# A PSUM ring kept through the next stage, whole first loads and one more weight buffer in a two-layer encoder step

## The chip, the cores and the metric

The kernel runs on one core of one Trainium2 chip. The metric is the time of one execution on the device in microseconds. Five engines matter: TensorE (PE, with PEld for its weight loads), VectorE (DVE), ScalarE (ACT), GpSimd (POOL) and SyncE (SP), which issues most DMAs. Each engine works through its own instructions strictly in the order in which the program gives them; semaphores hold an instruction until what it needs is there. The order on each engine is written by the kernel itself.

## The reference

One inference step of an encoder trunk of two layers, for 1024 prompt frames and 32 sample frames (1056 columns together), with model width 1024. All numbers are 32-bit floats.

```python
# layer 0
q, k, v, o, ig, fg = split(x @ w_in)
mix = mlstm(q, k, v, ig, fg) * g_norm * sigmoid(o) @ w_out      # 8 heads, chunks
x = layer_norm(alpha * x + mix)
x = layer_norm(alpha * x + (silu(x @ w_g) * (x @ w_u)) @ w_down)
# layer 1
k_sh, v_sh = x @ w_kv
mix = windowed_attention(x @ w_q, k_sh, v_sh, sinks, alibi) @ w_out   # 16 heads
x = layer_norm(alpha * x + mix)
x = layer_norm(alpha * x + (silu(x @ w_g) * (x @ w_u)) @ w_down)
```

The inner width of the SwiGLU layer is 2816. Outputs are x for both groups, the final states of the recurrence and the last window rows of keys and values.

## The kernel before

**Products.** A product of 32-bit numbers is made on TensorE from two halves of each operand: a rounded part (hi) and the rest (lo), with three matmuls per 128-row tile, hi x hi, hi x lo and lo x hi (`gemm`, lines 365 to 367). For weights the halves are called wh and wl, for activations both lie in `SX` (sx), with further room in `E` (ex). Columns are worked in three groups of 384, 384 and 288 (`GRP`) in the projections, and in four quarters of 264 (`QUARTERS`) around the layer norms and the SwiGLU layers.

**Weights.** The class `Weights` holds a list of units of 128 x 1024 numbers in order of use. Each unit is loaded by SP into one of three raw buffers (`wr`, `RAW`), then each of its two factors is split: ScalarE writes wh (line 206), and GpSimd, or VectorE for the factors in the set `on_vector`, writes wl (line 208). Split factors live in `SLOTS` buffers (tags wh and wl), except those that have a `home` elsewhere. `live` counts the buffers in use. `done` gives a factor's buffer back and splits on until `SLOTS - 1` are in use; where `ahead` is set, `feed` splits one more whenever a buffer is free and 1.7 us of planned matmul time have passed. After the last factor of a unit `load_to` orders the next raw load, on SP's queue at that place.

In the SwiGLU layers, pairs of units are combined: seven factors a1, a2, b2, s2, s1, s3, s4 come from two units and from sums of their parts that VectorE makes in place in the raw buffers (lines 179 to 185); each is used by 24 matmuls on sums of the activations. The seven products use them in the order a1, a2, s2, b2, s1, s3, s4. Up products (`up_tile`) add into bank pairs A and B of PSUM, which ScalarE copies out (lines 1356, 1366, 1373, 1384) and VectorE adds up (lines 1361, 1369, 1376 to 1378). The intermediate is split and stored to DRAM by `stage` (lines 1282 to 1284) and loaded back for the down products (`load`, line 1433). Down products (`down`) work through five blocks; VectorE adds each bank into `ACT` (act, the activations) at lines 1485 and 1487. `stage`, the loads and the norms are tasks (`Weave`) that advance with the planned time of the matmuls.

**The end of a SwiGLU layer.** The last block of the down product is plain: for each quarter eight products (`run` in `ffn`), each into one PSUM bank out of a ring of five (`dense_psum(5)`, `psbank`), added to act by VectorE at line 1547. Behind each quarter runs a layer norm task (`ln_task`): VectorE sums over tiles (lines 603 and 605), a matmul with a matrix of 1/1024 gives the mean (line 426), VectorE centres (431), ScalarE squares (433), VectorE and GpSimd sum up (435, 438), a second such matmul gives the variance (442), ScalarE takes logarithm, exponential and square (448 to 450), VectorE finishes the scale (452, 453), scales (456), ScalarE or VectorE apply gain and bias (464, 462) and the halves are made (470, 476). After the last quarter of layer 0 the norms of its third and fourth quarter are still running when the next stage begins.

**The next stage.** Layer 1 begins with the shared keys and values of the first column group (`keys_values(0)`: `k_group`, whose result ScalarE and VectorE split at lines 1581 and 1582, and `v_group`, line 1614) and four query projections (`q_group(j, 0)`, lines 1623 and 1624). Each takes one bank with `psbank`. In the kernel before, the ring of five is closed at the end of `ffn`, a ring of three opened, and two banks `psS` for the attention scores are taken right away, with a memset each (line 1661). The norm tasks hold three further banks on the other side of PSUM.

**The start.** SP loads the first half of the first weight unit (line 165), two of eight x tiles of the first column group (line 637), the second half (line 167), the other six, the second unit in halves, and then the other column groups (line 644). Each x tile is split by ScalarE and VectorE (lines 395 and 396). Twelve small matmuls run before (line 631). The first projections write q (ScalarE copies at line 697) and k, with a ring of three banks.

Of the kernel before, what the change touches and what calls it, by code (L numbers as in the profile page):

```python
# [9 lines left out]
F32 = mybir.dt.float32  # L10
# [3 lines left out]
PSUM = bass.MemoryType.PSUM  # L14
DRAM = bass.MemoryType.DRAM

P = 128
D = 1024
KT = D // P
# [21 lines left out]
NG = 2 * HEADS  # L41
WD = D + 4 * NG
RAW = 3
SLOTS = 5
GAP_M = (0.6, 1.666, 1.519, 1.5)
GAP_A = 0.46

# [15 lines left out]
GRP = ((0, 384), (384, 384), (768, 288))  # L63
# [65 lines left out]
class Weights:  # L129
# [21 lines left out]
                self.last[u] = len(self.jobs) - 1  # L151
                u += 1

    def load_to(self, i, between=None):
        while self.nload <= i and self.nload < len(self.units):
            u = self.nload
            ap = self.units[u]
            w = ap.shape[-1]
            r = self.pool.tile([P, WD], F32, name=f"wr{u}", tag="wr", bufs=RAW)
            self.raw[u] = r  # L160
            self.nload += 1
            if between is None:
                self.nc.sync.dma_start(r[:, :w], ap)
                continue
            self.nc.sync.dma_start(r[:, : w // 2], ap[:, : w // 2])
            between()
            self.nc.sync.dma_start(r[:, w // 2 : w], ap[:, w // 2 :])

    def _source(self, u, f):

# [17 lines left out]
    def _next(self):  # L188
# [3 lines left out]
        u, f = key  # L192
        if key not in self.home and len(self.live) == SLOTS:
            return False
# [7 lines left out]
        else:  # L202
            self.live.add(key)
            hi = self.pool.tile([P, WD // 2], F32R, name=f"wh{u}_{f}", tag="wh", bufs=SLOTS)[:, :w]
            lo = self.pool.tile([P, WD // 2], F32R, name=f"wl{u}_{f}", tag="wl", bufs=SLOTS)[:, :w]
        self.nc.scalar.copy(hi, r)  # L206
# [25 lines left out]
    def done(self, u, f=None):  # L232
        for k in (0, 1) if f is None else (f,):
            self.parts.pop((u, k))
            self.live.discard((u, k))
        while not self.ahead and len(self.live) < SLOTS - 1 and self.njob < len(self.jobs) and self._next():
            pass
# [9 lines left out]
def kernel(ctx: ExitStack, tc: tile.TileContext, A, O):  # L247
    nc = tc.nc
# [5 lines left out]
    def pool(name, space=None, side=None):  # L254
        kw = {}
        if space is not None:
            kw["space"] = space
        if side is not None:
            kw["side"] = side
        return tc.tile_pool(name=name, bufs=1, reuse_waits="tile", **kw)  # L260

    def new(p, tag, shape, dt=F32, bufs=1):
        uid[0] += 1
        return p.tile(list(shape), dt, name=f"{tag}_{uid[0]}", tag=tag, bufs=bufs)
# [6 lines left out]
    units, on_vector, pairs = [], set(), set()  # L271
# [12 lines left out]
    U_Q, U_K, U_V = [], [], []  # L284
# [31 lines left out]
    U_OUT_B = [[add("wout_b", u) for u in range(8)] for _ in range(2)]  # L316
    add_ffn(1)
    on_vector.update((u, f) for u in U_OUT_A[0] + U_OUT_B[1] for f in range(2))
    on_vector.update([(0, 0), (0, 1), (1, 0)])
    W = Weights(nc, base, units, pairs, on_vector)  # L320
    wv.feed = W.feed

# [16 lines left out]
    def views(t):  # L339

        return [[t[:, k, t0 : t0 + n] for t0, n in GRP] for k in range(KT)]

    act, sxh, sxl = views(ACT), views(SX[:, 0]), views(SX[:, 1])
# [5 lines left out]
    psx = [None, None]  # L349

    def dense_psum(bufs):
        psx[0] = ExitStack()
        psx[1] = psx[0].enter_context(pool("psd", PSUM)), bufs
# [16 lines left out]
    def psbank():  # L370
        return new(psx[1][0], "d", [P, 512], F32, bufs=psx[1][1])
# [22 lines left out]
    def split_act(k, g):  # L394
        nc.scalar.copy(sxh[k][g][:], act[k][g][:])  # L395
        nc.vector.tensor_sub(sxl[k][g][:], act[k][g][:], sxh[k][g][:].bitcast(F32))  # L396
# [194 lines left out]
    def norm_tail(li, run, box, final=False):  # L591


        tasks = []
        for g, (cols, (c, zs)) in enumerate(QUARTERS):

            def after(order, i):
                if i in (3, 5, 7):
                    if i == 3 and g > 1:
                        wv.drain(tasks[g - 2])  # L600
                    acc = box[0].z[:, 0:2, c, zs]
                    pair = [ACT[:, order[j] : order[j] + 2, cols] for j in (i - 1, 0)]
                    nc.vector.tensor_add(acc, acc if i > 3 else pair[1], pair[0])
                if i == KT - 1:
                    nc.vector.tensor_add(acc[:, 0], acc[:, 0], acc[:, 1])

            if final and g == 3:
                wv.drain(tasks[1])
                run(g, cols, None, LastNorm(box[0].z, box[0].lnps, QUARTERS[g], li))
                break  # L610
            run(g, cols, after)
            if g == 0 and li & 1:
                nc.scalar.preload_act_table_set("natural_log_exp_and_others")
            last = g >= 3
            tasks.append(wv.launch(ln_task(box[0].z, box[0].lnps, QUARTERS[g], li, last, final)))
            box[0].norms = tasks
        return tasks
# [13 lines left out]
        nc.tensor.matmul(warm[:, :P], onesm[:], onesm[:], start=True, stop=True)  # L631
    for g, (t0, n) in enumerate(GRP):
        if g == 0:

            def inputs(*ks):
                for k in ks:
                    nc.sync.dma_start(act[k][0][:], A["x"][:, k, : GRP[0][1]])

            W.load_to(0, lambda: inputs(0, 1))
            inputs(*range(2, KT))  # L640
            W.load_to(1, lambda: None)
        else:
            for k in range(0, KT, 2):
                nc.sync.dma_start(act_g[g][:, k : k + 2], A["x"][:, k : k + 2, t0 : t0 + n])
        if g == 2:
            W.load_to(2)
        if g == 0:
            gbias = pa.tile([40, 1], F32, name="gbias")
            sm0 = pa.tile([HEADS, 1], F32, name="sm0")
            nc.sync.dma_start(gbias[0:8], A["b_gate"][0:8])  # L650
            nc.sync.dma_start(gbias[32:40], A["b_gate"][8:16])
            nc.sync.dma_start(sm0[:], A["state_m"])
            gt = gp.tile([P, 9, NG], F32, name="gt")
            smask = gp.tile([HEADS, 384], F32, name="smask")
            sel = gp.tile([HEADS, PAIRS, P], F32, name="sel")
            cmask = pa.tile([P, P], F32, name="cmask")
            nc.sync.dma_start(smask[:], A["smask"])
            nc.sync.dma_start(ident[:], A["ident"])
    W.factor(0, 0)
    for g in range(3):  # L660
        for k in range(KT):
            split_act(k, g)
            if (g, k) == (0, 1):
                W.split_to(0)
        if g == 0:
            W.split_to(1)
    nc.sync.dma_start(sel[:], A["sel"])
# [564 lines left out]
    def ffn(layer, li, tasks, lx, final):  # L1232
# [283 lines left out]

        late = [(u, f) for u in dn[TAIL] for f in range(2)][SLOTS - 1 :]
        for b in range(TAIL):
# [11 lines left out]
        px.close()  # L1530
        W.ahead = True
        dense_psum(5)
        for _ in range(3):
            psbank()
        lx.lnps = lx.enter_context(pool("lnps", PSUM, side="right"))

        def run(g, cols, after, own=None):
# [13 lines left out]

        r = norm_tail(li, run, [lx], final)
        lx.ex.close()
        psx[0].close()
        dense_psum(3)
        return r

    def parts_made(g):
# [1 line left out]

    tasks, lx = mixer_out(U_OUT_A, 0, lx, None, lambda g: g < 3 and parts_made(g))
    tasks = ffn(0, 1, tasks, lx, False)

    eb = ExitStack()
    pb = eb.enter_context(pool("pb"))
    psb0 = eb.enter_context(pool("psb0", PSUM))
    psS = [psb0.tile([P, 512], F32, name=f"psS{h}") for h in range(2)]  # L1570
    KC = T + P
    KH = [pb.tile([P, KC], F32R, name=f"KH{g}") for g in range(2)]
    KL = [pb.tile([P, KC], F32R, name=f"KL{g}") for g in range(2)]
# [75 lines left out]
    def load_bias(j):  # L1649
        at, bufs = (pb2, 1) if j == 5 else (pb, 2)  # L1650
        bt = new(at, "bt", [P, 2, 257], bufs=bufs)
        sb = new(at, "sb", [DEC, 2, 161], bufs=bufs)
        nc.sync.dma_start(bt[:, :, 0:256], A["bias"][:, 2 * j : 2 * j + 2, :])
        nc.sync.dma_start(sb[:, :, 0:160], A["bias"][:DEC, 2 * j : 2 * j + 2, 0:160])
        nc.gpsimd.tensor_copy(bt[:, :, 256], nsink[:, 2 * j : 2 * j + 2])
        nc.gpsimd.tensor_copy(sb[:, :, 160], nsink[:DEC, 2 * j : 2 * j + 2])
        B[j] = (bt, sb)

    load_bias(0)
    for h in range(2):  # L1660
        nc.vector.memset(psS[h][:, 256:257], 0.0)
    def keys_values(g):
        if g == 2:
            k_part(ck[:], SEQ, P)
        for f, w in ((k_group, U_KV[g > 0][0]), (v_group, U_KV[g > 0][1])):
            f(g)
            if g != 1:
                W.done(w)
# [8 lines left out]
        wv.drain(t)  # L1677
    lx.close()
    lx.zx.close()

    pb2 = eb.enter_context(pool("pb2"))
    W.home[U_QB[1][5], 1] = [new(pb2, "oh", [P, D // 2], F32R, bufs=2)[:] for _ in range(2)]
# [177 lines left out]

    tasks, lx = mixer_out(U_OUT_B, 2, None, finish, before)
    ffn(1, 3, tasks, lx, True)
    while wv.tasks:
        wv.tick(0.25)
# [129 lines left out]
```

## Time and profile before

| | us |
|---|---|
| median of 3 runs | 2232.54 |
| lowest and highest | 2228.96, 2235.09 |
| the profiled execution | 2233.3 |
| its span, first to last instruction | 2231.5 |
| TensorE busy in it | 2184.5 |
| VectorE, ScalarE, GpSimd busy | 1452.1, 1000.8, 1042.2 |

Rows of a timeline give the start, the length, the engine, the line, the operation and the tiles (out<-in); rows that follow one another with the same form are merged (xN). In square brackets stands how long the engine was idle before it and what it waited for. In the list of waits each line has the waiting and the awaited operation, the total, the number of times and the longest. In the rows by stretch, each pair is busy time and number of instructions, and the granted clock is that of TensorE as a share of full speed. Matmuls overlap, so the length of a matmul row is longer than its distance to the next one.

### The profile page before, as it was taken

To read this page: it belongs to the slowest core of one execution; us is meant where nothing else is said; L and a number is where in the kernel's file an instruction comes from. 1 tells how busy PE (TensorE), PEld (TensorE's weight loads), DVE (VectorE), ACT (ScalarE), POOL (GpSimd) and SP (SyncE) were. 2 spreads that over 40 slices of the span, in tenths; PEclk is the share of its full clock that TensorE was granted. 3 is DMA by queue.
4 is the path that set the end of the run, shared out by engine and by line. 5 is a ranking of instruction groups with operands and counts; after the bars stand their busy time and mean duration, and the time that the engine had idled before them with its cause. 6 is when DMAs were issued, how large, how long until landed. Compare 5 with 4: busy or idle time off the path is not lost.

```text
span 2231.5 us, 44260 instructions
## 1 busy us (share of the span) xinstructions
PE 2184.5 (98%) x17086; PEld 2154.7 (97%) x17086; DVE 1452.1 (65%) x2833; ACT 1000.8 (45%) x2259; POOL 1042.2 (47%) x997
## 2 busy tenths in 40 slices
PE   9999999999999999999998999999999999999997
PEld 8899999999999999999998999899999999999997
DVE  4465577777566665566667678788666665456657
ACT  3443355455444444322235778756344444422225
POOL 2444331003666666544525776700566666554441
PEclk9999999999999999999999999999999999999999
DMA  4222112311443444697525433421244344398722
GB/s 150 74 55 66 51 38 93 98 39 58 165 139 141 154 145 144 217 331 237 177 69 168 115 103 86 141 79 40 100 167 155 134 144 157 125 332 270 238 72 79
DMA packets 174787, 298.10 MB, mean 134 GB/s; under 512 B 18096, under 2 KB 130792, under 8 KB 174576
## 3 DMA queue, kind: packets, MB, share of 16 engines
q1 hardware_dynamic: 170224, 290.94, 40.0%
q10 hardware_dynamic: 4352, 4.33, 0.6%
q8 instruction: 135, 2.21, 0.4%
q14 instruction: 76, 0.62, 0.1%
HBM read 201.80 MB, written 82.94 MB: 128 GB/s over the span
## 4 chain that ended last, share of the span: by engine, by line
PE 60%; DVE 5%; DMA 3%; ACT 3%; issue 2%; POOL 2%; SPq 0%; POOLq 0%; DVEq 0%; ACTq 0%
PE A L365 9%; PE A L367 9%; PE A L366 9%; PE B L365 6%; PE B L366 6%; PE B L367 6%; PE d L365 4%; PE d L367 4%; PE d L366 4%; DMA wr<-in_dn 1%; PE T L1759 1%; ACT act L464 1%; POOL s L1739 1%; PE O L1774 1%; PE O L1775 1%
## 5 line engine op out<-in xcount | busy, mean ns | idle before, releaser
L208 POOL TENSOR_TENSOR wl_s<-wr,wh_s 128x512 fp32r<-128x512 f32 x224 | 316.1, 1430 | 247.2 <-ACT wh_s L206 189.6
L365 PE MATMUL d<-sx,wh 128*128 128x264 f32 (+2 forms) x1068 | 343.4, 322 | 4.6 <-DVE act L1547 2.4
L367 PE MATMUL d<-sx,wl 128*128 128x264 f32 (+2 forms) x1068 | 326.9, 306 | 1.1 <-POOL wl L208 1.1
L366 PE MATMUL d<-sx,wh 128*128 128x264 f32 (+2 forms) x1068 | 326.7, 306 | 0.5 <-DVE sx L396 0.4
L208 POOL TENSOR_TENSOR wl_a<-wr,wh_a 128x512 fp32r<-128x512 f32 x112 | 168.3, 1510 | 327.7 <-ACT wh_a L206 325.6
L206 ACT CAST wh_s<-wr 128x512 fp32r<-128x512 f32 x224 | 135.6, 617 | 308.4 <-DVE wr L183 280.8
L365 PE MATMUL A<-sx,wh_s 128*128 128x264 f32 x896 | 254.9, 284 | 1.7 <-ACT z L1366 1.7
L366 PE MATMUL A<-sx,wh_s 128*128 128x264 f32 x896 | 254.2, 284 | 0.0
L367 PE MATMUL A<-sx,wl_s 128*128 128x264 f32 x896 | 254.0, 284 | 0.0
L365 PEld LDWEIGHTS d<-sx,wh 128*128 128x128 f32 x1068 | 203.3, 190 | 8.3 <-issue 2.6
L366 PEld LDWEIGHTS d<-sx,wh 128*128 128x128 f32 x1068 | 203.5, 191 | 2.5 <-DVE sx L396 1.5
L208 POOL TENSOR_TENSOR wl<-wr,wh 128x512 fp32r<-128x512 f32 (+2 forms) x94 | 123.1, 1318 | 177.1 <-ACT wh L206 174.5
L367 PEld LDWEIGHTS d<-sx,wl 128*128 128x128 f32 x1068 | 202.7, 190 | 2.0 <-POOL wl L208 1.7
L365 PE MATMUL d<-sx,ex 128*128 128x264 f32 x624 | 180.6, 289 | 0.4 <-ACT sx L395 0.2
L366 PE MATMUL d<-sx,ex 128*128 128x264 f32 x624 | 177.4, 284 | 0.4 <-DVE sx L396 0.2
L367 PE MATMUL d<-sx,ex 128*128 128x264 f32 x624 | 176.9, 284 | 0.0
L365 PEld LDWEIGHTS A<-sx,wh_s 128*128 128x128 f32 x896 | 168.4, 188 | 2.4 <-ACT z L1366 2.1
L367 PEld LDWEIGHTS A<-sx,wl_s 128*128 128x128 f32 x896 | 168.9, 188 | 0.0
L366 PEld LDWEIGHTS A<-sx,wh_s 128*128 128x128 f32 x896 | 168.4, 188 | 0.0
L1283 POOL TENSOR_TENSOR z<-z 128x528 fp32r<-128x528 f32 x76 | 104.4, 1373 | 110.4 <-ACT z L1282 103.7
L1739 POOL TENSOR_SCALAR s<-s,st 128x256 f32<-128x256 f32 (+1 forms) x144 | 123.0, 866 | 44.3 <-DVE st L1737 30.4
L1282 ACT CAST z<-z 128x528 fp32r<-128x528 f32 x136 | 85.8, 631 | 94.3 <-DVE z L1295 40.5
(347 smaller groups left out, 7292.7 us busy)
## 6 DMA issues: line engine op xcount, KB each, us to landing
wr<-in_gu SPq DMA_DIRECT2D x92, 512.0 KB
hs_x<-z SPq DMA_DIRECT2D x72, 528.0 KB
hs_t<-z SPq DMA_DIRECT2D x64, 528.0 KB
sx<-hs_x SPq DMA_DIRECT2D x112, 264.0 KB
sx<-hs_t SPq DMA_DIRECT2D x64, 264.0 KB
ex<-hs_t SPq DMA_DIRECT2D x64, 264.0 KB
wr<-in_dn SPq DMA_DIRECT2D x32, 512.0 KB
ex<-hs_x SPq DMA_DIRECT2D x32, 264.0 KB
```

What stands on the lines that cost most here:

```text
L206: self.nc.scalar.copy(hi, r)
L208: eng.tensor_sub(lo, r, hi.bitcast(F32))
L365: nc.tensor.matmul(out, ah, bh, start=start and k == 0, stop=False, **kw)
L366: nc.tensor.matmul(out, ah, bl, start=False, stop=False, **kw)
L367: nc.tensor.matmul(out, al, bh, start=False, stop=stop and k == last, **kw)
L464: nc.scalar.activation(z, z, AF.Identity, scale=gk, bias=bk)
L1282: nc.scalar.copy(hi.bitcast(F32R), buf(s))
L1283: eng.tensor_sub(lo.bitcast(F32R), buf(s), hi)
L1739: nc.gpsimd.tensor_scalar_mul(p[:R, h, lo:256], p[:R, h, lo:256], st[:R, 2, h : h + 1])
L1759: nc.tensor.transpose(pt[:nk, i, h, :R], p[:R, h, c : c + nk], ident[:R, :R])
L1774: nc.tensor.matmul(po[:, :, :R], v, s["hi"][:nk, i, :, :R], start=(i == 0), stop=False)
L1775: nc.tensor.matmul(po[:, :, :R], v, s["lo"][:nk, i, :, :R], start=False, stop=(i == len(kts) - 1))
```

## The change

Three edits go together.

- The ring of five banks is no longer closed at the end of `ffn`. It stays through the first key, value and query projections, and is closed after the norm tasks are done; then the ring of three is opened and `psS` taken and set. The three calls of `psbank` whose result nothing uses are gone.
- The first two weight units are each loaded by one DMA, the first ahead of all eight x tiles, the second behind them. Both factors of the first unit are split before the first x tile is. On VectorE are now the two factors of the first unit; the first factor of the second unit moves to GpSimd.
- `SLOTS` goes from 5 to 6: six buffers for wh and six for wl. With it `done` keeps five in use, and in the last block of the down product five factors, not four, lie in these buffers while one fewer gets a place in `E` (line 1517).

```diff
-SLOTS = 5
+SLOTS = 6
...
-    def load_to(self, i, between=None):
+    def load_to(self, i):
         while self.nload <= i and self.nload < len(self.units):
...
+            self.nc.sync.dma_start(r[:, :w], ap)
             self.raw[u] = r
             self.nload += 1
-            if between is None:
-                self.nc.sync.dma_start(r[:, :w], ap)
-                continue
-            self.nc.sync.dma_start(r[:, : w // 2], ap[:, : w // 2])
-            between()
-            self.nc.sync.dma_start(r[:, w // 2 : w], ap[:, w // 2 :])
...
-    on_vector.update([(0, 0), (0, 1), (1, 0)])
+    on_vector.update((u, f) for u in U_Q[:1] for f in range(2))
...
-            W.load_to(0, lambda: inputs(0, 1))
-            inputs(*range(2, KT))
-            W.load_to(1, lambda: None)
+            W.load_to(0)
+            for k in range(KT):
+                nc.sync.dma_start(act[k][g][:], A["x"][:, k, t0 : t0 + n])
+            W.load_to(1)
...
-    W.factor(0, 0)
+    W.split_to(0)
     for g in range(3):
         for k in range(KT):
             split_act(k, g)
-            if (g, k) == (0, 1):
-                W.split_to(0)
         if g == 0:
             W.split_to(1)
...
         dense_psum(5)
-        for _ in range(3):
-            psbank()
         lx.lnps = lx.enter_context(pool("lnps", PSUM, side="right"))
...
         lx.ex.close()
-        psx[0].close()
-        dense_psum(3)
         return r
...
-    psb0 = eb.enter_context(pool("psb0", PSUM))
-    psS = [psb0.tile([P, 512], F32, name=f"psS{h}") for h in range(2)]
...
-    for h in range(2):
-        nc.vector.memset(psS[h][:, 256:257], 0.0)
...
     lx.close()
     lx.zx.close()
+    psx[0].close()
+    dense_psum(3)
+    psb0 = eb.enter_context(pool("psb0", PSUM))
+    psS = [psb0.tile([P, 512], F32, name=f"psS{h}") for h in range(2)]
+    for h in range(2):
+        nc.vector.memset(psS[h][:, 256:257], 0.0)
```

More of the change, by code (lines that the diff above doesn't have):

```diff
@@ L633 @@
         if g == 0:
-            def inputs(*ks):
-                for k in ks:
-                    nc.sync.dma_start(act[k][0][:], A["x"][:, k, : GRP[0][1]])
-            W.load_to(0, lambda: inputs(0, 1))
-            inputs(*range(2, KT))
-            W.load_to(1, lambda: None)
+            W.load_to(0)
+            for k in range(KT):
+                nc.sync.dma_start(act[k][g][:], A["x"][:, k, t0 : t0 + n])
+            W.load_to(1)
         else:
```

## The prediction

> **What bounds the kernel now.** I read the page first, then the list of waits, then busy time by stretch, and last the timelines around each long wait of TensorE.
>
> ```profile
> span 2231.5 us, 44260 instructions
> PE 2184.5 (98%) x17086; PEld 2154.7 (97%) x17086; DVE 1452.1 (65%) x2833; ACT 1000.8 (45%) x2259; POOL 1042.2 (47%) x997
> ```
>
> TensorE is idle for 2231.5 - 2184.5 = 47 us. The change removes no matmul, so it can win only some of that, and the slow matmuls that follow a long pause. The waits name what it can reach:
>
> ```profile
> PE A L365 <- DVE act L1485: 3.3, 2, 1.7
> PE ln L442 <- DVE z L438: 2.8, 1, 2.8
> PE d L365 <- DVE act L1547: 2.4, 1, 2.4
> PE d L365 <- ACT qT L697: 1.8, 1, 1.8
> PE d L367 <- POOL wl L208: 1.1, 2, 0.6
> ...
> ACT wh_b L206 <- DMA wr<-in_dn: 21.7, 6, 4.5
> ...
> ACT wh_b L206 <- DMA wr<-in_gu: 6.9, 6, 2.0
> ```
>
> Columns: total us, times, longest. The third line is the PSUM bank that the first key projection waits for, the second the layer norm behind it, the first the start of the second down product, the fifth a weight half that came late. The stretches say where there is nothing to win, and what a pause costs afterwards:
>
> ```profile
> 560.00:960.00 400.00, 398.72 (x3280) 1.00 0.47 166
> ...
> 20.00:24.00 4.00, 2.18 (x13) 1.85 (x12) 2.52 (x7) 3.17 (x8) 2.14 (x6) 1.00 0.93 339
> 1182.00:1184.50 2.50, 2.50 (x9) 2.40 (x9) 1.20 (x4) 0.00 (x0) 0.00 (x0) 0.50 0.27 89
> 1203.80:1208.00 4.20, 4.14 (x12) 3.96 (x13) 0.82 (x2) 2.29 (x5) 2.27 (x2) 0.50 0.39 124
> ```
>
> In the up products of one layer (first row: length, TensorE busy, matmuls, granted clock) 1.3 us of 400 are idle, at 400 / 3280 = 0.122 us a matmul, so 24 of them, one weight factor, take 2.9 us. In the last two rows the clock is at 0.50 after a pause; across the 1.82 us pause of the second row it stayed at 1.00.
>
> **Part 1: the ring of five banks.** Around the end of layer 0's last down product:
>
> ```profile
> 1173.93 0.42 DVE L1547 TENSOR_TENSOR act<-act,d 128x264 f32<-128x264 f32 x1
> ...
> 1179.04 0.71 DVE L435 TENSOR_TENSOR z<-z 128x528 f32<-128x528 f32 x1 [1.18 <-POOL z L435]
> 1179.78 0.43 DVE L438 TENSOR_TENSOR z<-z 128x264 f32<-128x264 f32 x1
> ...
> 1181.21 0.76 DVE L1547 TENSOR_TENSOR act<-act,d 128x264 f32<-128x264 f32 x2
> 1181.78 0.66 PE L365 MATMUL d<-sx,wh 128*128 128x384 f32 x1 [2.37 <-DVE act L1547]
> ...
> 1182.75 0.43 DVE L605 TENSOR_TENSOR z<-z 128x264 f32<-128x264 f32 x1
> ...
> 1183.84 1.08 PE L442 MATMUL ln<-z,onesm 128*128 128x264 f32 x2
> 1184.96 0.48 ACT L448 ACTIVATE z<-ln,eps_ln 128x264 f32<-128x264 f32 x1 [7.86 <-PE ln L442]
> ...
> 1185.44 0.34 PE L365 MATMUL d<-sx,wh 128*128 128x384 f32 x1
> ...
> 1185.62 0.34 PE L366 MATMUL d<-sx,wh 128*128 128x384 f32 x1
> ...
> 1186.39 0.49 DVE L452 SCALAR_TENSOR_TENSOR z<-ln,eps_ln,z 128x264 f32<-128x264 f32 x1 [3.14 <-ACT z L450]
> ...
> 1188.60 0.61 PE L426 MATMUL ln<-z,onesm 128*128 128x264 f32 x2
> ...
> 1188.78 0.56 DVE L1582 TENSOR_TENSOR KL<-d,KH 128x384 fp32r<-128x384 f32 x1 [0.69 <-ACT KH L1581]
> ...
> 1199.25 3.05 DVE L435 TENSOR_TENSOR z<-z 128x528 f32<-128x528 f32 x2
> ...
> 1201.70 4.38 POOL L208 TENSOR_TENSOR wl<-wr,wh 128x512 fp32r<-128x512 f32 x3
> 1202.34 1.38 DVE L438 TENSOR_TENSOR z<-z 128x264 f32<-128x264 f32 x1
> ...
> 1203.86 1.22 PE L442 MATMUL ln<-z,onesm 128*128 128x264 f32 x2 [2.85 <-DVE z L438]
> ```
>
> TensorE finished the last product at 1181.78 - 2.37 = 1179.41 and then waited for the first of the last two additions (1181.21 x2), that of the seventh product of eight. So bank 0 of the new ring of three is the seventh product's, although line 1533 takes three banks beforehand: those three are written by nothing and the trace shows no turn of the ring by them (with it bank 0 would be that of the fourth product). In the kept ring of five without them, 32 products have gone round, and the key projection gets the bank of the fourth product, whose addition started at 1173.93. The 2.37 us go.
>
> What is late next? TensorE runs one 384-wide matmul per (1185.62 - 1185.44) = 0.18 us. It reaches the variance matmul (L442) after 6 of them, at 1179.41 + 1.06 = 1180.5; its input is the L438 that ends at 1179.78 + 0.43 = 1180.2. So it is not held, where today it stands at 1183.84. ScalarE's three steps follow 1.1 us behind and take 1.4 us, so they end at 1183.0 and VectorE goes from L605 (ends 1183.18) straight to L452: the idle 3.14 us vanish. The projection ends near 1179.41 + 24 x 0.175 + 0.45 = 1184.1 instead of 1188.6, and with it the 0.69 us before L1582. VectorE's chain is then 3.14 + 0.69 = 3.8 us early, TensorE 4.5. Both meet again at the second L442 (1203.86), whose input comes from VectorE: TensorE's wait grows from 2.85 to about 3.5 us, and 3.8 us remain. The slow clock after it stays as it is. Bounds: nothing, if VectorE's chain is held elsewhere; at most 4.5 + 2.85 and the slow clock behind the second pause (13 matmuls at 0.32 instead of 0.18, 1.9 us), 9.2 us. I take **-3.8**. The two memsets of psS (0.06 us each) move behind the projections on VectorE, where only the first scores wait for them: nothing.
>
> **Part 2: first loads whole.**
>
> ```profile
> 0.72 0.40 SPq L165 DMA_DIRECT2D wr<-in_wqk  x1
> ...
> 3.81 0.62 ACT L206 CAST wh<-wr 128x512 fp32r<-128x512 f32 x1 [1.81 <-DMA wr<-in_wqk]
> ...
> 6.65 0.62 ACT L206 CAST wh<-wr 128x512 fp32r<-128x512 f32 x1 [0.55 <-DMA wr<-in_wqk]
> ...
> 17.04 4.76 ACT L395 CAST sx<-act 128x384 fp32r<-128x384 f32 x12 [1.97 <-DMA act<-in_x]
> ...
> 22.23 0.44 PE L365 MATMUL d<-sx,wh 128*128 128x384 f32 x1 [1.82 <-ACT qT L697]
> ```
>
> The first half (256 KB) is there at 3.81; two x tiles and the second half (640 KB) follow in 2.84 us, so a whole first unit costs 256 / 225 = 1.1 us more and is there near 4.95. Then two casts (0.62 each) and both subtractions stand ahead of the first x tile, and the first matmul starts about 1.5 us later than now. From the third x tile on the bytes that must have come are the same, two DMA issues fewer, and the first projection ends some 0.3 us late; the second unit's first half, subtracted on GpSimd instead of VectorE, adds about 0.6. All of that runs into the 1.82 us that TensorE waits at 22.23 for a copy behind 12 casts of x, and those wait for x itself, which does not come later. Cover gone, it would cost the 0.9. A wider pause might drop the clock (24 matmuls slower by 0.145, 3.5 us, of which 1.8 are covered). Bounds -0.5 (fewer issues ahead of x) to +2.6; I take **+0.4**.
>
> [...]
>
> **Part 3: the sixth buffer.** One weight factor more is split ahead; no split is added. The wait for wl in the projections (0.53 of the 1.1 us) should go: **-0.5**, between -1.1 and 0. In the up products there is nothing to win. At the start of the second down product there is:
>
> ```profile
> 944.97 0.62 ACT L206 CAST wh_s<-wr 128x512 fp32r<-128x512 f32 x1
> 952.84 0.63 ACT L1282 CAST z<-z 128x528 fp32r<-128x528 f32 x1 [7.25 <-DMA hs_x<-z]
> 953.38 0.61 ACT L206 CAST wh_s<-wr 128x512 fp32r<-128x512 f32 x1
> ...
> 955.30 1.92 SPq L163 DMA_DIRECT2D wr<-in_dn  x2
> ...
> 962.48 0.69 DVE L179 TENSOR_TENSOR wr<-wr,wr 128x512 f32<-128x512 f32 x1 [0.38 <-DMA wr<-in_dn]
> ```
>
> The last cast of a pair (953.38) stands behind a cast that waits 7.25 us for a store; only when its raw buffers are free can the next loads be issued (955.30), and L179 waits for them ahead of the last additions of the product, which hold TensorE for 1.65 us, once in each layer. With six buffers that last cast takes the place of the one at 944.97, in front of the blocked one, the loads go out some 4 us earlier, and L179 stands one factor (2.9 us) earlier, ahead of additions whose bank isn't wanted next. Best -3.3; if the loads do not move, L179 blocks one more set of additions (two at 0.7) and it is +2.8 for both layers. I take half of the gain, **-1.65**. On SP's queue the x loads behind move back by these two issues (1.9 us with their wait).
>
> **Sum:** -3.8 + 0.4 - 0.5 - 1.65 = -5.5 us. The profiled execution took 2233.3 us (span 2231.5 and 1.8 around it), 0.8 above the median 2232.54 of the three runs; from the median the forecast is 2227.0 us, -0.25%.
>
> **Rivals.**
>
> Faster still: the second pause shrinks too. Between 1199 and 1204 VectorE's L435 and L438 take 3.05 for two and 1.38, where 0.71 and 0.43 are their usual times; three subtractions of GpSimd run beside them. If one factor ahead moves these away, VectorE's chain is 1.6 + 0.95 = 2.6 us shorter. With both downs won (-3.3) and both wl waits (-1.1): -3.8 - 2.6 - 3.3 - 1.1 = -10.8, 2221.7 us. Against it: the splits keep their spacing, and as many are due there.
>
> No gain: the sixth factor's subtraction (1.3 us or more) falls into the same norm beside VectorE's sums, and makes them slower as the three do now: 2.6 us back, and the downs don't move: -3.8 - 0.5 + 2.6 + 0.4 = -1.3, 2231.2 us. [...] Also here belongs that the ring isn't what holds the key projection: then its 3.8 us stay.
>
> Slower: in ScalarE's queue. The cast of b2, which waits for its load (wh_b: 21.7 + 6.9 = 28.6 us over 12 times), stood ahead of the SiLU that ends a tile; one factor earlier it stands ahead of the copy (L1373) that TensorE needs within 2.9 us. It decides from the point where the second raw unit of a pair comes more than one factor after that copy could run. If half of these 28.6 us reach TensorE, +14.3 against -3.8: +10.5, 2243.0 us. For it: ScalarE and VectorE take their work strictly in turn. Against it: the loads are ordered one factor earlier too.
>
> **How the numbers follow.** Forecast 0.43, the faster rival 0.27, no gain 0.15, slower 0.15. From no change a measurement here tells about 0.3%, 6.7 us, so below 2225.8 is faster: the faster rival and a third of the forecast's own range (2224 to 2230.5), 0.27 + 0.14 = 0.41. Slower is the last rival, 0.15; 0.44 lies between. The range 2219 to 2236 takes in all but the slower rival and a tail of some 0.05.
>
> **What would show it.** Right: no wait of L365 on L1547 near 1180, VectorE without the 3.14 us before L452, the second L442 still waiting, some 3.5 us, and about 3.8 us earlier; no wait of A on L1485; the first real matmul near 6.6 us but the pause before the fourth projection shorter by as much. Wrong: a new wait of A on the copy at L1373 in the up products, a clock of 0.50 in the first 15 us, or VectorE's sums before L438 slower than 3.05 and 1.38 us.

## The result, and the profile after

The changed kernel takes 2240.4 us (median of 6 runs, 2237.9 to 2243.4) against 2229.4 us for the kernel before on the same chip (6 runs, 2226.5 to 2235.1): ratio 1.0044, 95% interval 1.0033 to 1.0054. It is slower by about 0.4%, outside the range of the prediction. The profiled execution took 2241.7 us. Lines of the changed kernel are those of before less 5 (up to line 633), less 11 (from 665 to 1532) and less 13 to 19 behind that.

From the page of the changed kernel, the span and the busy times of the engines:

```profile
span 2239.8 us, 44269 instructions
PE 2188.3 (98%) x17086; PEld 2159.7 (96%) x17086; DVE 1476.0 (66%) x2832; ACT 1009.2 (45%) x2259; POOL 1028.1 (46%) x998
```

As many matmuls as before; TensorE is idle for 51.5 us instead of 47, and busy for 3.8 us longer: both are to be explained. The waits of TensorE after (total us, times, longest):

```profile
PE A L360 <- ACT wh_s L201: 12.9, 14, 3.1
PE ln L437 <- DVE z L433: 5.6, 2, 4.7
...
PE A L360 <- ACT wh_b L201: 0.9, 1, 0.9
...
PE d L362 <- POOL wl L203: 0.4, 1, 0.4
```

Of the waits shown of before, those on the additions L1547 (2.4) and on the copy L697 (1.8) are gone, the wait for wl fell from 1.1 to 0.4, and the second layer norm wait grew from 2.8 to 4.7. New is the first line: 14 waits, 7 in each layer, where before had 2 of 3.3 us in all. All 14 stand at the change from one down product to the next (8 products in four blocks, so 7 changes a layer). ScalarE's cast, which the line names, isn't what is late: here is the second of these changes, first TensorE, then VectorE (start, length, engine, line, operation, tiles, idle before).

```profile
981.50 0.28 PE L362 MATMUL A<-sx,wl_s 128*128 128x264 f32 x1
...
982.32 0.37 PE L360 MATMUL A<-ex,wh_a 128*128 128x264 f32 x1 [0.54 <-ACT wh_s L201]
```

```profile
977.42 2.78 DVE L1476 TENSOR_TENSOR act<-act,B 128x528 f32<-128x528 f32 x4
980.12 0.68 DVE L177 TENSOR_TENSOR wr<-wr 128x512 f32<-128x512 f32 x1
980.91 0.69 DVE L178 TENSOR_TENSOR wr<-wr,wr 128x512 f32<-128x512 f32 x1
981.52 1.31 DVE L1474 SCALAR_TENSOR_TENSOR act<-act,A 128x528 f32<-128x528 f32 x2
```

TensorE starts on a1 of the next product at 982.32, as the first of the two additions L1474 ends (981.52 + 0.70 = 982.2). Those are the additions of s4, the last factor. A down product keeps both bank pairs A until s4 is added, so a1 of the next one can begin only when the first of them is added. Ahead of these additions VectorE now makes the two sums of s2 for a later unit (L177, L178). The same place before:

```profile
980.20 2.76 DVE L1487 TENSOR_TENSOR act<-act,B 128x528 f32<-128x528 f32 x4 [0.75 <-PE B L367]
982.88 0.69 DVE L179 TENSOR_TENSOR wr<-wr,wr 128x512 f32<-128x512 f32 x1
983.49 0.70 DVE L1485 SCALAR_TENSOR_TENSOR act<-act,A 128x528 f32<-128x528 f32 x1
984.57 0.70 DVE L1485 SCALAR_TENSOR_TENSOR act<-act,A 128x528 f32<-128x528 f32 x1 [0.38 <-PE A L367]
985.19 0.68 DVE L182 TENSOR_TENSOR wr<-wr 128x512 f32<-128x512 f32 x1
985.98 0.69 DVE L183 TENSOR_TENSOR wr<-wr,wr 128x512 f32<-128x512 f32 x1
```

One sum (L179) stood ahead of the additions, and the sums of s2 (L182, L183) came behind them. VectorE even waited 0.38 us for the second bank: TensorE ended s4 near 984.5, the first bank was free at 984.2, some 0.3 us to spare. One VectorE operation of 0.7 us more, and TensorE waits.

At the first change of each layer the delay is largest:

```profile
951.89 0.71 DVE L1272 TENSOR_TENSOR z<-z 128x528 fp32r<-128x528 f32 x1 [4.55 <-ACT z L1271]
...
953.75 1.22 DVE L174 TENSOR_TENSOR wr<-wr,wr 128x512 f32<-128x512 f32 x1
954.89 2.53 DVE L1476 TENSOR_TENSOR act<-act,B 128x528 f32<-128x528 f32 x4
957.35 0.68 DVE L177 TENSOR_TENSOR wr<-wr 128x512 f32<-128x512 f32 x1
958.13 0.69 DVE L178 TENSOR_TENSOR wr<-wr,wr 128x512 f32<-128x512 f32 x1
958.74 1.31 DVE L1474 SCALAR_TENSOR_TENSOR act<-act,A 128x528 f32<-128x528 f32 x2
```

VectorE has stood for 4.55 us behind the last staging of the up products and then works without a pause. In this backlog stand three operations on weights ahead of the additions of s4, the difference L174 and the two sums, where before had one (L179): TensorE waits 3.11 us at 959.58 (before: 1.65). And the clock then falls. Rows by stretch (length, busy time and number of matmuls, weight loads, VectorE, ScalarE, GpSimd, granted clock, DMA), after the 3.11 us pause and after a 0.54 us one:

```profile
959.50:963.20 3.70, 3.62 (x20) 3.65 (x21) 2.64 (x3) 1.07 (x3) 3.60 (x3) 0.65 1.09 369
982.30:986.00 3.70, 3.68 (x30) 3.70 (x31) 3.04 (x4) 1.64 (x4) 3.62 (x3) 1.00 0.03 7
```

20 matmuls instead of 30 in 3.7 us, which is 1.2 us more; until the clock is back it is 1.5, as 15 matmuls start 0.220 us apart instead of 0.122. Where the span went can be read off by pairing the matmuls of the two kernels one by one and taking the difference of their starts (after less before, worked out from the two traces):

| matmul, at us of before | after less before | the stage up to there |
|---|---|---|
| 104 | -5.8 | projections and first of the recurrence of layer 0 |
| 958 | -6.8 | rest of layer 0, almost up to its second down product |
| 1087 | +2.1 | the combined down products of layer 0: +8.9 |
| 1186 | -0.8 | last block and first key projection: -2.9 |
| 1230 | +2.1 | second norm behind it: +2.9 |
| 1997 | +0.3 | layer 1 up to its second down product: -1.8 |
| 2143 | +8.2 | the combined down products of layer 1: +7.9 |

The down products lose 16.8 us, more than everything else wins. Of the 8.9 in layer 0 the waits give: six at 0.7 (from the rows above, 982.32 - 981.50 = 0.82 between starts instead of the usual 0.12), 4.2; 3.11 instead of 1.65, 1.5; the single wait of 0.9 at 953.3, about 1.0; the clock 1.5. That is some 8.2 of 8.9.

The norm behind the last down product, VectorE and GpSimd, answers to the rows around 1179 and 1186 of before:

```profile
1181.20 1.77 DVE L430 TENSOR_TENSOR z<-z 128x528 f32<-128x528 f32 x1 [1.18 <-POOL z L430]
...
1186.34 0.48 DVE L447 SCALAR_TENSOR_TENSOR z<-ln,eps_ln,z 128x264 f32<-128x264 f32 x1
```

```profile
1181.13 1.28 POOL L203 TENSOR_TENSOR wl<-wr,wh 128x512 fp32r<-128x512 f32 x1
```

L447 (L452 before) no longer waits for ScalarE, as foretold for the ring; but a subtraction of GpSimd now starts beside VectorE's sum, which takes 1.77 us instead of 0.71. In the norm behind it the same happens once more: a subtraction starts on GpSimd at 1197.33, and VectorE's first sum takes 1.83 us, where it takes 0.69 in `e2_ring` below.

```profile
1197.36 1.83 DVE L430 TENSOR_TENSOR z<-z 128x528 f32<-128x528 f32 x1
```

In the first 25 us, ScalarE, SP and TensorE:

```profile
4.20 1.14 ACT L201 CAST wh<-wr 128x512 fp32r<-128x512 f32 x2 [2.21 <-DMA wr<-in_wqk]
...
16.19 2.27 ACT L390 CAST sx<-act 128x288 fp32r<-128x288 f32 x6 [0.18 <-DMA act<-in_x]
18.36 0.47 ACT L686 COPY qT<-d 128x384 f32<-128x384 f32 x1
```

```profile
7.78 4.94 SPq L635 DMA_DIRECT2D act<-in_x  x8
```

```profile
5.81 0.44 PE L360 MATMUL d<-sx,wh 128*128 128x384 f32 x1
```

The whole first unit is there at 4.20, and the first matmul of the projections starts at 5.81 (before: 5.16). The x tiles of the later groups are issued from 7.78 on (before: 9.69), ScalarE is through with the casts of x and goes on to the copy at 18.36 instead of 21.70, and TensorE's pause of 1.82 us ahead of the fourth projection is gone.

### The profile page after: what moved, and what is told of

Its sections match the earlier page's. It is cut to its first block, busy times and chain, and to the rows that moved or that the text cites. A ratio compares the mean times of both kernels' runs of the same rounds, so it can differ in the third digit from the quotient of the medians.

```text
span 2239.8 us, 44269 instructions
## 1 busy us (share of the span) xinstructions
PE 2188.3 (98%) x17086; PEld 2159.7 (96%) x17086; DVE 1476.0 (66%) x2832; ACT 1009.2 (45%) x2259; POOL 1028.1 (46%) x998
## 3 DMA queue, kind: packets, MB, share of 16 engines
q10 hardware_dynamic: 4352, 4.33, 0.6%
## 4 chain that ended last, share of the span: by engine, by line
PE 81%; DVE 8%; ACT 5%; POOL 2%; DMA 2%; issue 2%; SPq 0%; DVEq 0%; POOLq 0%; ACTq 0%
PE A L360 10%; PE A L361 9%; PE A L362 9%; PE d L360 8%; PE d L362 8%; PE d L361 8%; PE B L362 7%; PE B L360 7%; PE B L361 7%; PE T L1746 1%; POOL wl L203 1%; ACT act L459 1%; POOL s L1726 1%; PE O L1761 1%; PE O L1762 1%
## 5 line engine op out<-in xcount | busy, mean ns | idle before, releaser
L360 PE MATMUL d<-sx,wh 128*128 128x264 f32 (+2 forms) x1092 | 350.0, 320 | 0.1
L361 PE MATMUL d<-sx,wh 128*128 128x264 f32 (+2 forms) x1092 | 333.0, 305 | 0.4 <-DVE sx L391 0.4
L362 PE MATMUL d<-sx,wl 128*128 128x264 f32 (+2 forms) x1092 | 332.7, 305 | 0.4 <-POOL wl L203 0.4
L203 POOL TENSOR_TENSOR wl_a<-wr,wh_a 128x512 fp32r<-128x512 f32 x112 | 151.1, 1356 | 366.6 <-ACT wh_a L201 365.5
L360 PEld LDWEIGHTS d<-sx,wh 128*128 128x128 f32 x1092 | 207.1, 190 | 2.9 <-ACT sx L390 0.2
L361 PEld LDWEIGHTS d<-sx,wh 128*128 128x128 f32 x1092 | 207.3, 190 | 1.7 <-DVE sx L391 0.7
L360 PE MATMUL d<-sx,ex 128*128 128x264 f32 x600 | 172.8, 288 | 0.4 <-ACT sx L390 0.2
L361 PE MATMUL d<-sx,ex 128*128 128x264 f32 x600 | 170.6, 284 | 0.6 <-DVE sx L391 0.6
L362 PE MATMUL d<-sx,ex 128*128 128x264 f32 x600 | 170.1, 284 | 0.0
L362 PE MATMUL A<-ex,wl_s 128*128 128x264 f32 x448 | 127.5, 285 | 0.0
```

What stands on the lines that cost most here:

```text
L203: eng.tensor_sub(lo, r, hi.bitcast(F32))
L360: nc.tensor.matmul(out, ah, bh, start=start and k == 0, stop=False, **kw)
L361: nc.tensor.matmul(out, ah, bl, start=False, stop=False, **kw)
L362: nc.tensor.matmul(out, al, bh, start=False, stop=stop and k == last, **kw)
```

## The experiments

Theory after this reading: the sixth buffer makes all of the loss, because the factor that `done` splits when s3 is given back is now s2, whose two sums stand on VectorE ahead of s4's additions; ring and first loads win. Rivals: the loss is a clash of the three edits, or of six buffers by themselves (other places in memory, other timing of GpSimd), and not of VectorE's order.

**The parts alone.** Four kernels on one chip, 26 runs of the kernel before beside them (median 2230.66 us).

`e1_slots`, the sixth buffer alone, in the kernel before:

```diff
-SLOTS = 5
+SLOTS = 6
```

> The kernel before with six split buffers and nothing else. Theory (the sixth buffer moves the pair sums of s2, lines 182 and 183, ahead of the additions of the s4 product on VectorE, in each of the eight down products of a layer): the whole loss of the two down stages comes back, some 9 us in layer 0 and 8 in layer 1, less 2 to 5 us that the earlier splits win elsewhere: +10 to +15 us against the kernel before, ratio 1.0045 to 1.0067, with TensorE waits of about 0.55 to 0.6 us at the start of 6 or 7 down products a layer. Rival (the loss lies in the ring or the first loads): within 3 us of before.

Measured: 2243.7 us, ratio 1.006 (1.0047 to 1.0073).

`e2_ring`, the ring alone:

```diff
-        for _ in range(3):
-            psbank()
...
-        psx[0].close()
-        dense_psum(3)
         return r
...
-    psb0 = eb.enter_context(pool("psb0", PSUM))
-    psS = [psb0.tile([P, 512], F32, name=f"psS{h}") for h in range(2)]
...
     lx.zx.close()
+    psx[0].close()
+    dense_psum(3)
+    psb0 = eb.enter_context(pool("psb0", PSUM))
+    psS = [psb0.tile([P, 512], F32, name=f"psS{h}") for h in range(2)]
```

> The kernel before with the ring of five kept through the first projections and nothing else. Theory: the wait of 2.37 us on the bank of the seventh product goes, part of it comes back as a longer wait on the variance input; -1 to -4 us, ratio 0.998 to 0.9996. The step of the prediction says -3.8. Rival (the ring loses): slower by 3 us or more.

Measured: 2226.87 us, ratio 0.998 (0.9971 to 0.999).

`e3_loads`, the first loads alone, with their places on VectorE:

```diff
-            W.load_to(0, lambda: inputs(0, 1))
-            inputs(*range(2, KT))
-            W.load_to(1, lambda: None)
+            W.load_to(0)
+            for k in range(KT):
+                nc.sync.dma_start(act[k][g][:], A["x"][:, k, t0 : t0 + n])
+            W.load_to(1)
...
-    W.factor(0, 0)
+    W.split_to(0)
```

> The kernel before with the first two units loaded whole, split as in the change, and nothing else. Theory: the x tiles of the second and third column group come 3 us earlier, so the wait of 1.82 us before the fourth projection goes: -1 to -3 us, ratio 0.9987 to 0.9996. The prediction's step says +0.4. Rival (whole loads delay the start by more than the cover): slower by 1 us or more.

Measured: 2228.59 us, ratio 0.9989 (0.998 to 0.9998).

`e4_five`, the changed kernel with five buffers again, that is ring and loads together:

```diff
-SLOTS = 6
+SLOTS = 5
```

> The changed kernel with five split buffers: ring and whole loads stay. Theory: the sum of the two parts alone, -2 to -7 us against the kernel before, ratio 0.997 to 0.999, and no waits of 0.55 us in the down products. Rival (six buffers are not the cause): 2238 to 2243 us as the changed kernel.

Measured: 2225.25 us, ratio 0.9975 (0.9965 to 0.9985).

The loss is the sixth buffer's: alone it costs 0.6%, and without it the other two win about what they win singly (0.2% and 0.11%, together 0.25%). No clash is needed. Waits of TensorE in `e1_slots`:

```profile
PE A L365 <- ACT wh_s L206: 13.2, 14, 3.3
...
PE d L365 <- DVE act L1547: 3.4, 1, 3.4
```

The same 14 waits, with the ring of before. In `e4_five` they are back to two:

```profile
PE A L360 <- DVE act L1474: 3.4, 2, 2.1
```

**The order on VectorE.** Four kernels on another chip, 17 runs of before beside them (2231.36 us). In `e5_ahead4` there are six buffers, but `done` splits no further ahead than with five:

```diff
-        while not self.ahead and len(self.live) < SLOTS - 1 and self.njob < len(self.jobs) and self._next():
+        while not self.ahead and len(self.live) < SLOTS - 2 and self.njob < len(self.jobs) and self._next():
```

> The changed kernel with six buffers, but giving a factor back splits on only until four are in use, as with five buffers; where the feed runs ahead, six may be in use. Theory (the loss comes from the split that runs one factor further ahead in the down products, not from the buffer): the 13 or 14 waits of 0.55 us and more are gone, and the 4 us that six buffers win in the first layer stay: 2217 to 2224 us, ratio 0.9945 to 0.9975. Rival (a sixth buffer costs by where it puts the tiles in SBUF): 2230 us or more. Beside it: with six buffers TensorE's matmuls of the up products in layer 0 stand 121.91 ns apart, with five 121.52; if the addresses do that, 121.9 here, if the further split, 121.5.

Measured: 2227.0 us, ratio 0.9984 (0.9975 to 0.9993). The 14 waits are gone (L1474: 3.1 us, 2 times), so these come from the lookahead and not from the buffer; but the gain over before is smaller than was expected.

`e6_held` keeps the lookahead of the change and only moves one release: the buffer of s3 is given back behind s4's additions, so that what it splits comes behind them on VectorE.

```diff
+                if f == "s3":
+                    continue
+                if f == "s4":
+                    W.done(u, "s3")
                 W.done(u, f)
```

> The changed kernel with one difference in the down products: factor s3 is given back behind the additions of s4, so that VectorE makes the sums of s2 (lines 177 and 178) after these additions and not ahead of them. Theory (order on VectorE): the waits of 0.55 to 0.6 us at the start of 12 down products go, and the two of some 3 us shrink; 2224 to 2232 us, ratio 0.9975 to 1.001. Rival (the order on VectorE is not it, the sixth buffer's split load is): within 3 us of the changed kernel, 2237 to 2243.

Measured: 2224.3 us, ratio 0.9974 (0.9963 to 0.9985). No buffer is added or taken and the same factors are split; with two VectorE operations behind the additions instead of ahead of them, the kernel goes from 0.44% slower than before to 0.26% faster. The edit moves the whole release, so ScalarE's cast and GpSimd's subtraction of that factor move with the sums. That VectorE's additions are what TensorE waits for is read from the rows of the change above.

`e7_pulled` does the harm without the buffer: the kernel before, five buffers, with one more factor split where s3 is given back.

```diff
                 W.done(u, f)
+                if f == "s3":
+                    W._next()
```

> The kernel before, with five buffers, and one more split when s3 is given back in the down products, so that the sums of s2 (lines 182 and 183) stand ahead of the additions of s4 as in the changed kernel. Theory: waits of 0.5 us and more at the start of 12 to 14 down products without any sixth buffer; +8 to +15 us against before, ratio 1.0035 to 1.0067. Rival (buffer or split load): within 3 us of before.

Measured: 2257.98 us, ratio 1.0122 (1.0109 to 1.0136), much more than was expected. VectorE at the same change of products as above:

```profile
986.39 0.69 DVE L179 TENSOR_TENSOR wr<-wr,wr 128x512 f32<-128x512 f32 x1
987.11 0.69 DVE L182 TENSOR_TENSOR wr<-wr 128x512 f32<-128x512 f32 x1
987.91 0.69 DVE L183 TENSOR_TENSOR wr<-wr,wr 128x512 f32<-128x512 f32 x1
988.52 1.31 DVE L1485 SCALAR_TENSOR_TENSOR act<-act,A 128x528 f32<-128x528 f32 x2
```

```profile
PE A L365 <- ACT wh_s L206: 24.4, 14, 4.2
```

Here three operations stand ahead of the additions, one more than in the change: the one of before and the two of s2. The same 14 waits, longer.

`e8_five_held`, five buffers, ring, loads, and the release of s3 behind the additions, takes away the one operation that stood there before, too:

```diff
-SLOTS = 6
+SLOTS = 5
...
+                if f == "s3":
+                    continue
+                if f == "s4":
+                    W.done(u, "s3")
                 W.done(u, f)
```

> Ring kept and loads whole with five buffers, and in the down products s3 given back behind the additions of s4, so that also the difference of line 174, which waits for a load, stands behind them. Theory: the two waits on line 1474 (3.4 us in all) go: 2220 to 2224 us, 1 to 4 us under the kernel with five buffers alone. Rival (the splits then come too late, as two factors start together): TensorE waits for wl in the down products, 2226 us or more.

Measured: 2222.74 us, ratio 0.9964 (0.9952 to 0.9977), the best kernel here beside `e9_pad` below; it beats both kernels of the case.

```profile
980.75 0.70 DVE L1474 SCALAR_TENSOR_TENSOR act<-act,A 128x528 f32<-128x528 f32 x1
982.22 0.70 DVE L1474 SCALAR_TENSOR_TENSOR act<-act,A 128x528 f32<-128x528 f32 x1 [0.76 <-PE A L362]
982.84 0.69 DVE L174 TENSOR_TENSOR wr<-wr,wr 128x512 f32<-128x512 f32 x1
983.56 0.69 DVE L177 TENSOR_TENSOR wr<-wr 128x512 f32<-128x512 f32 x1
```

```profile
PE A L360 <- DVE act L1474: 1.2, 2, 0.6
```

The sums stand behind both additions. Put together, at the six later changes of a layer the wait follows the number of operations that stand between the additions of s3 and those of s4. The first is covered, the second makes a wait of some 0.55 us and the third adds some 0.75, with five buffers as with six:

| operations of 0.7 us ahead of s4's additions | kernel | wait at the first change of a layer | at each of the six others |
|---|---|---|---|
| 0 | `e8_five_held` | 0.6 | none |
| 0 | `e6_held` | 1.6 to 1.7 | none |
| 1 | before | 1.65 | none |
| 1 | `e5_ahead4` | 1.5 to 1.6 | none |
| 2 | the change | 2.9 to 3.1 | 0.54 to 0.60 |
| 2 | `e1_slots` | 3.0 to 3.3 | 0.54 to 0.60 |
| 3 | `e7_pulled` | 4.1 to 4.2 | 1.3 to 1.7 |

The first change does not follow this count, because there all of VectorE's backlog behind the late staging counts. In `e6_held` the difference of line 174 still stands in it, ahead of the additions of s3:

```profile
953.52 1.24 DVE L174 TENSOR_TENSOR wr<-wr,wr 128x512 f32<-128x512 f32 x1
```

So there `e6_held` has one operation on weights, like before, and the change has three. `e7_pulled` has three too and waits longer, as one of them (L182) takes 1.76 us there.

**What six buffers cost beside that.** `e5_ahead4` and `e6_held` stayed some 0.1% above their likes with five buffers (`e4_five`, `e8_five_held`), though the intervals overlap. Part of this is waits: `e6_held` waits 2.2 us longer than `e8_five_held` at the two first changes, and both kernels have the second norm wait of 4.7 us, where their likes have 2.8. Another part lies in the up products. The stretch 600 to 800 us, in which TensorE never waits, of the change and of before:

```profile
600.00:800.00 200.00, 200.00 (x1643) 200.00 (x1642) 123.74 (x133) 86.25 (x151) 116.24 (x88) 1.00 0.40 146
```

```profile
600.00:800.00 200.00, 200.00 (x1648) 200.00 (x1647) 126.36 (x134) 83.42 (x151) 126.25 (x88) 1.00 0.42 148
```

Five matmuls fewer at the full clock: 200 / 1643 = 0.1217 us each against 0.1214. By the starts of some 2,500 matmuls of that stage it is 121.91 against 121.52 ns; in the up products of layer 1 it is 121.72 against 121.43. Two kernels built on `e8_five_held`, on a third chip with 16 runs of before (2229.7 us), ask whether the place in memory of what lies behind the buffers does it, or six buffers taken in turn.

`e9_pad` leaves 4352 bytes a partition unused behind the five buffers (by the order of allocation; no trace shows the addresses):

```diff
+    pad = base.tile([P, 2 * (WD // 2)], F32, name="pad")
+    nc.gpsimd.memset(pad[:, :1], 0.0)
```

> The kernel of the run before (five buffers, ring kept, whole loads, s3 held back) with 4352 unused bytes a partition behind the split buffers, as much as a sixth pair takes, so that all that lies above moves by as much. In every run with six buffers the matmuls of the up products of layer 0 stand 121.91 ns apart, in every run with five 121.52. Theory (addresses of what lies above, E among it): 121.9 ns, and some 2 to 4 us slower than without the bytes. Rival (use of the sixth buffer or more traffic): 121.5 ns and the same time.

Measured: 2222.64 us, ratio 0.9971 (0.996 to 0.9983).

`e10_sixth_idle` has six buffers in turn with never more than five in use:

```diff
-            hi = self.pool.tile([P, WD // 2], F32R, name=f"wh{u}_{f}", tag="wh", bufs=SLOTS)[:, :w]
-            lo = self.pool.tile([P, WD // 2], F32R, name=f"wl{u}_{f}", tag="wl", bufs=SLOTS)[:, :w]
+            hi = self.pool.tile([P, WD // 2], F32R, name=f"wh{u}_{f}", tag="wh", bufs=SLOTS + 1)[:, :w]
+            lo = self.pool.tile([P, WD // 2], F32R, name=f"wl{u}_{f}", tag="wl", bufs=SLOTS + 1)[:, :w]
```

> The same kernel with five factors in use at most, but six buffers in turn for wh and for wl. Theory (addresses): 121.9 ns between the matmuls of the up products of layer 0, 2 to 4 us slower than with five. Rival (the split that runs further ahead): 121.5 ns and the same time.

Measured: 2224.64 us, ratio 0.9978 (0.9969 to 0.9987). The same stretch of `e9_pad`, then of `e10_sixth_idle`:

```profile
600.00:800.00 200.00, 200.00 (x1648) 200.00 (x1647) 124.91 (x134) 85.31 (x154) 126.32 (x89) 1.00 0.42 146
```

```profile
600.00:800.00 200.00, 200.00 (x1643) 200.00 (x1642) 126.38 (x133) 85.26 (x155) 127.85 (x90) 1.00 0.41 146
```

All five kernels with six buffers (the change, `e1_slots`, `e5_ahead4`, `e6_held`, `e10_sixth_idle`) have 1643 matmuls in this stretch, and all seven with five (before, `e2_ring`, `e3_loads`, `e4_five`, `e7_pulled`, `e8_five_held`, `e9_pad`) have 1648. So it is neither the lookahead (`e5_ahead4` has that of before), nor what lies behind the buffers (`e9_pad`), nor more factors in use (`e10_sixth_idle`), but the six buffers themselves. Whether their addresses or the turn of six does it stays open; that wasn't tried. In time it is small: 0.39 ns for the 3,360 matmuls of the up products of layer 0 and 0.29 ns for as many in layer 1 would be 2.3 us, and the intervals of `e9_pad` and `e10_sixth_idle` overlap.

## Why the prediction was wrong

**The sixth buffer in the down products** (-1.65 forecast, worst +2.8) is the step that failed: "L179 stands one factor (2.9 us) earlier, ahead of additions whose bank isn't wanted next". For L179 that came true: it is L174 in the rows of after, now behind the second addition of s1, and the raw loads did go out earlier (at 945.02; the offset of the two traces makes that 951.8 on the clock of before, where it was 955.30). But L179 isn't the only VectorE instruction that a factor further ahead moves. The two sums of s2 follow it at one factor's distance, and they stepped from behind s4's additions to ahead of them, into the one place of a down product where the next product waits for a bank. The prediction followed the instruction that it saw in a wait, and not each that the step issues. Its worst case, "L179 blocks one more set of additions", was sized for one change of products in each layer, where there are seven, and left out the clock behind the longer pause: 16.8 us in place of 2.8.

**The ring** (-3.8) was right in kind and nearly in size: alone 0.2%, 4.5 us of 2230.66, and by the starts of the matmuls 3.6 us at the first key projection. In `e2_ring` the wait for L1547 is gone and VectorE goes straight from L605 to L452:

```profile
1182.53 0.43 DVE L605 TENSOR_TENSOR z<-z 128x264 f32<-128x264 f32 x1
1182.88 0.49 DVE L452 SCALAR_TENSOR_TENSOR z<-ln,eps_ln,z 128x264 f32<-128x264 f32 x1
```

```profile
1199.60 1.22 PE L442 MATMUL ln<-z,onesm 128*128 128x264 f32 x2 [2.84 <-DVE z L438]
```

The second norm wait did not grow to the 3.5 us foretold; it stayed at 2.84. In the changed kernel it grew to 4.71, and the 2.9 us won there were lost again by 1230. That is the place of the rival "no gain": the sixth factor's subtraction beside VectorE's sums, 1.77 us where 0.71 was usual. In the kernel before, three of VectorE's 37 sums of this line (L435) took 1.18, 1.32 and 1.63 us, each with subtractions of GpSimd beside it for 0.6 us or more, and the other 34 took 0.69 to 0.71. That the subtraction alone made the wait of 4.71 wasn't tried. It goes with the sixth factor in use: the four kernels in which six can be in use (the change, `e1_slots`, `e5_ahead4`, `e6_held`) all have 4.7, `e4_five` has 2.8, and `e10_sixth_idle`, six buffers with five in use, has 1.1.

**The first loads** (+0.4) had the wrong sign: alone 0.11% faster, 2.5 us of 2230.66. The first unit came at 4.20 and not at 4.95, and "x itself, which does not come later" was costed at no more than -0.5: the later x tiles are issued 1.9 us earlier, the casts of x end 3.3 us earlier, and the 1.82 us pause, the cover of this term, was itself won (0.24 in `e3_loads`). The clock stayed at 1.00 in the first 15 us.

**The waits for wl** (-0.5) went as foretold, 1.1 to 0.4 us, but elsewhere the sixth buffer won more than the prediction allowed it. By 104 us `e1_slots` is 4.1 us ahead of before: of TensorE's waits there, 0.57 us at 65.20 (wl), 1.23 at 96.61 (line 899) and 1.59 at 104.22 (line 966), 3.4 us in all, are gone in it and in the change. In the up products, where there was "nothing to win", before waits 1.28 us at 585.68 for line 1366, and the change doesn't. What made these waits of the recurrence and of line 1366 go was not tried.

**The slower rival** named the right part and about the right time (2243.0), by another mechanism: ScalarE's cast of b2 ahead of the copy in the up products. No wait of A on that copy appeared, and in the changed kernel the up products have no wait of A at all. Its ground, "ScalarE and VectorE take their work strictly in turn", bore on the other engine and in the other stage: in the rows of the change VectorE makes the two sums at 957.35 and 958.13 and then the addition at 958.74, for which TensorE waited 3.11 us.

**The clock.** In the prediction's rows the clock stayed at 1.00 across a pause of 1.82 us and was at 0.50 after one of 2.37 us. The length of the pause alone does not decide it. In the same trace 0.50 also follows pauses of 1.24 us (at 1242.18) and 1.44 us (at 1433.50), which stand among other waits of the attention. In `e1_slots` the clock fell behind a pause of 3.28 us (at 960.40; mean 0.59 over the next 3.6 us), and behind one of 3.04 us (at 2002.42) it was at 1.00:

```profile
2002.40:2006.00 3.60, 3.58 (x30) 3.60 (x30) 2.91 (x4) 1.49 (x3) 3.56 (x3) 1.00 1.07 367
```

Behind pauses of 2.94, 3.11 and 4.71 us in the changed kernel it was at 0.50 as well. From which length on a pause brings the clock down was not shown.

## What to carry to other kernels

When a queue is made deeper, write down every instruction that each job issues on every engine, place them all one job earlier, and ask of each which instruction it now stands ahead of, and whether that one frees a bank or buffer that is wanted at once. Where an order is written by hand, give a buffer back behind the critical instructions and not where its last reader stands: one moved release took the changed kernel from 0.44% slower to 0.26% faster. And where a wait is put down to an engine that had long finished, look for the instruction that ended just then: here the list named ScalarE's cast 14 times, and it was VectorE's addition.

## What the hardware showed beside that

- In the up products of layer 0 matmuls of 264 columns stand 121.91 ns apart with six weight buffers in turn and 121.52 with five, with TensorE never idle and the clock at 1.00; all five kernels with six have 1643 of them in the 200 us from 600 on, all seven with five 1648. The cause is open.
- Pauses of 2.94 and 3.11 us in the changed kernel were each followed by 15 matmuls 0.220 us apart instead of 0.122. In `e1_slots` 19 matmuls started in 3.6 us behind a pause of 3.28 us, and 30 behind one of 3.04 us; after the 3.28 us:

```profile
960.40:964.00 3.60, 3.60 (x19) 3.60 (x20) 2.44 (x3) 0.98 (x2) 3.58 (x3) 0.59 1.08 366
```

  So a pause that passes from 1.65 to 3.1 us costs 1.5 us itself and, where the clock falls, 1.2 to 1.5 more after it.
- With whole loads in place of halves the eight x loads of the later groups were issued 1.9 us earlier, with two issues fewer ahead.
